# Storing residual tiles later, and two units in seven products for two more up projections, in a two-layer hybrid trunk

## The chip, the cores and the metric

The kernel runs on one core of a Trainium2 chip. The metric is the time of one execution on the device in microseconds (us). A measurement is the median of several runs; the profile is of one further execution, taken by the hardware profiler.

## The reference

Two layers work on 256 tokens of width 2048, all in float32. Each layer normalises x, projects it to queries, keys, values, the two halves of a spatial gating unit and two sets of gates, runs sliding-window attention and the gating unit, projects both to the model width, merges them with the gates, projects once more and adds the result to x. Then comes a gated feed-forward block of width 5632, added to x as well:

```python
for l in range(DEPTH):
    h = rms_norm(x, mix_norm[l])
    proj = h @ w_in[l]
    q, k, v, uv, gate_logits = jnp.split(proj, cuts, axis=-1)
    ...
    merged = gates[..., :D_MODEL] * branch_a + gates[..., D_MODEL:] * branch_b
    x = x + merged @ w_out[l]
    h2 = rms_norm(x, ffn_norm[l])
    x = x + (jax.nn.silu(h2 @ w_gate[l]) * (h2 @ w_up[l])) @ w_down[l]
```

## The kernel before

**Precision.** TensorE multiplies in a rounded format, so each operand is split into a high part (the rounded value) and a low part (the remainder), and a product is three matmuls: high by high (L399), weight's low by activation's high (L400), weight's high by activation's low (L401). For a weight block of 256 rows by 512 columns, ScalarE makes the high part (`whi`, L256) and VectorE the low part (`wlo`, L264). The activations are stored transposed in four units of 512 rows (`uh`, `ul`).

**Jobs and steps.** A job is one product of all 256 tokens with 1024 weight columns (two halves of 512, c = 0 and c = 1). It goes over its units; a whole step is one weight block against both token tiles, 12 matmuls, so a unit has 4 steps, 48 matmuls. The first `m` units of a job instead take a Strassen-like scheme: seven products of 6 matmuls, 42 in all. It costs four subtractions of weight blocks (L240, VectorE), seven high and seven low parts in place of four, and sums of activation blocks (`sh`, `sl`), which a unit has only if it was made with `sums`. `HEAD` says which products come first in a job (five for m = 1, nine for m = 2: 11a, 11b, t1a, t1b, t2a, t2b, 21a, t3a, t3b), `TAIL` which are mixed into the whole steps, and `SUM_AT` how many steps ahead of the job each subtraction is made.

**The order of the work** is written out by hand: nothing is scheduled by the compiler, and every engine takes its instructions in the order in which the program emits them. `Stream.next` keeps the high parts up to six and the low parts up to five blocks ahead of TensorE, emits the subtractions when their step has come, and emits the load of a weight buffer (1 MB, SP's queue, L220) as soon as the blocks of the buffer five loads earlier have been used. `after(n, fn)` puts work n steps later; a whole step counts 1, a product 0.5. `evicting` empties the accumulators behind a job's half, the second token tile some steps later, which depends through `behind` on the `m` of the next job.

**Residuals and norms.** `residual` (L967 on) runs two jobs whose halves are the four tiles of x, each 256 by 512. Each tile is fetched ahead (`fetch_x`, SP's queue, L356); behind its half VectorE adds the product to it (L995 or L997) and the tile is stored to DRAM for the next residual (`keep_x`, 512 KB, SP's queue, L359), 7 steps behind the first half of a job or 8 behind the second. Where a norm follows (both output projections, and the last down round of layer 0), the tile also becomes a unit of the next stage: VectorE transposes it in blocks (L483), POOL issues 16 gathers of 32 KB (L489, at most eight under way), ScalarE scales what has landed (L583) and makes its high part (L587, or L511 and L523 with sums), VectorE its low part (L590). The gathers of one tile stand behind those of the tile before on POOL's queue.

**The feed-forward block** has three rounds over hidden tiles 0 to 3, 4 to 7 and 8 to 10. A round takes a gate and an up job for each pair of hidden tiles (named by the pair's first tile: gate 0, up 0, gate 2, up 2 and so on), then two down jobs. The gate's half is evicted by ScalarE (L1088), the up half by VectorE (L1094), which multiplies both; the hidden tile is then transposed by the same gathers. Gate 2, 4, 6 and 8 have m = 2, gate 0 and all up and down jobs m = 1. Where this text numbers a layer's jobs, gate 0 follows the second job of the output projection. All larger tiles share 25 buffers (`N_BIG`).

Of the kernel before, what the change touches and what calls it, by code (L numbers as in the profile page):

```python
# [37 lines left out]
N_BIG = 25  # L38
G_BUSY, G_LAND = 3.5, 3
T1_LATE, THEN_LATE, UNIT_LATE = (1.5, 3), (3, 7), (3, 3)  # L40
Q_FIRST = 15
Q_STEP = 4
LOAD_BY = (1, 2, 3, 4)
ROUNDS = ((0, 1, 2, 3), (4, 5, 6, 7), (8, 9, 10))
M_OUT, M_FFN, M_DOWN = (0, 1), (2, 1, 1), 1
M_Q = 0
M_GATE, M_ATT, M_SGU = (1, 1, 1, 1), (0, 0), (1, 0)
M_V, M_U = 1, 1
# [4 lines left out]
def hybrid_trunk(ctx: ExitStack, tc: tile.TileContext, x, mix_norm, w_in, q_norm, k_norm, sinks,  # L53
# [106 lines left out]
    for l in range(DEPTH):  # L160
        wl = w_in[l]
        for o in (0, None)[::-1 if l == 0 else 1]:
            add_job([wl[:, o:o + CW2]], m=M_Q * l) if o is not None else add_job([wl[:, O_KV:O_KV + CW]])
        for o, m in ((O_V, M_V), (O_U, M_U), (O_GATE, M_GATE[0]), (O_GATE + CW2, M_GATE[1])):
            add_job([wl[:, o:o + CW2]], m=m)
        add_job([wl[:, O_GATE + D:O_GATE + D + CW2]], m=M_GATE[2])
        for i, o in enumerate((0, CW2)):
            add_job([w_attn_branch[l, :, o:o + CW2]], m=M_ATT[i])
        add_job([wl[:, O_GATE + D + CW2:O_GATE + 2 * D]], m=M_GATE[3])
        for i, o in enumerate((0, CW2)):  # L170
            add_job([w_sgu_branch[l, :, o:o + CW2]], m=M_SGU[i])
        for i, o in enumerate((0, CW2)):
            add_job([w_out[l, :, o:o + CW2]], m=M_OUT[i])
        for fs in ROUNDS:
            for f in fs[::2]:
                if f + 1 < NF:
                    for w, m in zip((w_gate, w_up), M_FFN if f else (1, 1)):
                        add_job([w[l, :, f * CW:(f + 2) * CW]], m=m)
                else:
                    add_job([w[l, :, f * CW:(f + 1) * CW] for w in (w_gate, w_up)], m=M_FFN[2])  # L180
            for o in (0, CW2):
                add_job([w_down[l, :, o:o + CW2]], units=list(fs), m=M_DOWN)

    needed = {}
    for i, n in uses:
# [109 lines left out]
    def after(n, fn):  # L295
        steps.append((slot_no[0] + n, fn))
# [61 lines left out]
    def keep_x(c):  # L358
        nc.sync.dma_start(rows(kept[c]), xt[c])  # L359
        home[c] = kept[c]  # L360
# [608 lines left out]
    def residual(units, nxt, sums, out_at=None, scale=None):  # L969

        for j in range(0, NCH, 2):

            def done(c, ps, j=j):
                o = j + c

                square_at = 5 if c == 0 else behind(2, 2, 5)

                def then():
                    nxt.unit(o, sums=o < sums)
                    after(square_at, lambda: nxt.squares(o))  # L980
                    if o == NCH - 1:
                        after(square_at + 1, lambda: nxt.finish())

                evicting(c, lambda t: added(o, t, ps), then if nxt is not None else None, late_then=UNIT_LATE)
                if out_at is None:
                    after(7 if c == 0 else 8, lambda: keep_x(o))

            def added(o, t, ps):
                n = 2 if out_at is not None and o == NCH - 1 else 1
                w = CW // n  # L990
                for i in range(n):
                    sl = slice(i * w, (i + 1) * w)
                    d, src = xt[o][:, t, sl], ps[t][:, sl]
                    if scale is None:
                        nc.vector.tensor_tensor(out=d, in0=src, in1=d, op=ALU.add)  # L995
                    else:
                        nc.vector.scalar_tensor_tensor(out=d, in0=src, scalar=scale, in1=d, op0=ALU.mult, op1=ALU.add)  # L997
                    if out_at is not None:
                        eng = nc.sync if i == 0 else nc.scalar
                        eng.dma_start(out_at[0, t * P:(t + 1) * P, o * CW + i * w:o * CW + (i + 1) * w], d)  # L1000

            job = jobs[job_no[0]]
            length = 3.5 * job.m + 4 * (len(job.units) - job.m)
            after(length - 8, lambda j=j: fetch_x(j))
            after(length - 6, lambda j=j: fetch_x(j + 1))
            run(units, done)
# [3 lines left out]
    for l in range(DEPTH):  # L1010

        pl = layer[l]
        parameters(pl)
        kv = slot([P, NT, CW], name="kv")
        qs = [slot([P, NT, CW], name="q") for _ in range(2)]
        att, spa = Attention(pl), Spatial(pl, norm)

        def scaled_into(c, dst, ps):
            evicting(c, lambda t: None,
                     ahead=lambda t: nc.scalar.activation(dst[:, t, :], ps[t], AF.Copy, scale=norm.r[t]))  # L1020

        def kv_done(c, ps):
            scaled_into(0, kv, ps)
            att.keys(kv)
            if l:
                att.begin()

        def q_done(c, ps):
            scaled_into(c, qs[c], ps)
            att.queries(c, qs[c])  # L1030
            if c == 1 and not l:
                att.begin()

        after(2, lambda unit=norm.units[0]: add_sums(unit))
        for done in (kv_done, q_done)[::-1 if l else 1]:
            run(norm.units, done)
        run(norm.units, spa.v)
        run(norm.units, spa.u)

        ga, gb, mT = [None] * NCH, [None] * NCH, [None] * NCH  # L1040

        def gate(dst, j):
            def done(c, ps):
                dst[j + c] = slot([P, NT, CW], name="gate")
                def tanh(t):
                    nc.scalar.activation(dst[j + c][:, t, :], ps[t], AF.Tanh, scale=norm.rh[t])

                evicting(c, lambda t: None, ahead=tanh)
            run(norm.units, done)

        def branch(dst, j, units, then=None):
            def done(c, ps):
                d = dst[j + c]

                def then_():
                    then(j + c)
                    transposed(mT, j + c, ga[j + c], sums=j + c == 0)

                evicting(c, lambda t: nc.vector.scalar_tensor_tensor(out=d[:, t, :], in0=d[:, t, :], scalar=1.0,
                                                                     in1=ps[t], op0=ALU.add, op1=ALU.mult),  # L1060
                         then_ if then is not None else None)
            run(units, done)

        def merge(j):
            nc.vector.tensor_tensor(out=flat(ga[j]), in0=flat(ga[j]), in1=flat(gb[j]), op=ALU.add)

        for j in (0, 2):
            gate(ga, j)
        gate(gb, 0)
        for j in (0, 2):  # L1070
            branch(ga, j, att.attT)
        after(SGU_SUMS, lambda unit=spa.sguT[0]: add_sums(unit))
        gate(gb, 2)
        for j in (0, 2):
            branch(gb, j, spa.sguT, merge)

        norm = Norm(ffn_cols(l))
        residual(mT, norm, max(M_FFN), scale=0.5)

        nxt = Norm(mix_cols(l + 1)) if l + 1 < DEPTH else None  # L1080
        for i, fs in enumerate(ROUNDS):
            hid, hT = {}, {}

            def gate_done(f, c, ps):
                hid[f] = a = slot([P, NT, CW], name="hid")

                evicting(c, lambda t: None,
                         ahead=lambda t: nc.scalar.activation(a[:, t, :], ps[t], AF.Silu, scale=norm.r[t]))  # L1088

            def up_done(f, c, ps):  # L1090
                a = hid[f]

                def upped(t):
                    nc.vector.scalar_tensor_tensor(out=a[:, t, :], in0=ps[t], scalar=norm.r[t], in1=a[:, t, :],  # L1094
                                                   op0=ALU.mult, op1=ALU.mult)

                evicting(c, upped, lambda: transposed(hT, f, a, on_pe=f == NF - 1, sums=f in fs[:M_DOWN]))

            for f in fs[::2]:
                if f + 1 < NF:  # L1100
                    run(norm.units, lambda c, ps: gate_done(f + c, c, ps))
                    run(norm.units, lambda c, ps: up_done(f + c, c, ps))
                else:
                    run(norm.units, lambda c, ps: (gate_done, up_done)[c](f, c, ps))
            if i == len(ROUNDS) - 1:
                if nxt is not None:
                    prepare(l + 1)
                residual(hT, nxt, M_Q, out if nxt is None else None)
            else:
                residual(hT, None, 0)  # L1110
        norm = nxt
# [37 lines left out]
```

## Time and profile before

| | |
|---|---|
| median of 3 runs | 2463.84 us (2461.32 to 2466.27) |
| the profiled execution | 2466.55 us |
| its span, first to last instruction | 2464.6 us |
| granted TensorE clock, mean | 0.997 |
| TensorE matmuls, of them in jobs | 10950, 10404 |
| VectorE busy | 1990.1 us, 81% |
| ScalarE busy | 1429.3 us, 58% |
| read from and written to HBM | 492.04 MB, 16.78 MB |

In the views of the profile PE is TensorE, DVE VectorE, ACT ScalarE, POOL GpSimd and SP SyncE; a `q` behind an engine is its queue. A line of a timeline has the start and the duration in us, engine, line, operation, what it writes and reads, how many alike follow each other, and in brackets how long the engine was idle before it and what ended that. A matmul is shown as 0.39 us long, but they overlap: one begins every 0.227 us. A line of the windows has, for a stretch A:B, its length, the busy time of each engine with the number of its instructions, the granted clock as a share of full speed (PEclk), the busy share of the 16 DMA engines and GB/s. "to landing" is the time from the issue of a DMA to the arrival of all its data.

### The profile page before, as it was taken

How to read it: one execution, taken by the hardware profiler on the slowest of the kernel's cores; microseconds unless marked ns; L12 is line 12 of the kernel's file. 1: busy time of each engine (PE TensorE's matmuls, PEld its weight loads, DVE VectorE, ACT ScalarE, POOL GpSimd, SP SyncE). 2: the span in 40 equal slices, each digit the busy share in tenths (PEclk: the TensorE clock that was granted, in tenths of full speed). 3: DMA queues.
4: the chain of work that ended last, by engine and by line, in shares of the span. 5: the costliest groups of instructions: out<-in, count | busy, mean ns of one | idle time of the engine just before them, and what ended most of it. 6: DMA issues, size and time to landing. Idle time of an engine off the chain costs nothing. (4 is left out here: it accounts for less than half of the span.)

```text
span 2464.6 us, 30889 instructions
## 1 busy us (share of the span) xinstructions
PE 2443.4 (99%) x10950; PEld 2012.3 (82%) x10950; DVE 1990.1 (81%) x2189; ACT 1429.3 (58%) x1758; POOL 475.0 (19%) x903
## 2 busy tenths in 40 slices
PE   9999999999999999999999999999999999999999
PEld 7888888877888888888888888887778888888887
DVE  7898768786978797788879976777869787978786
ACT  6575545475655665465666665554756555655653
POOL 1421300441220022002235022014402200220020
PEclk9999999999999999999999999999999999999999
DMA  8555556776576757666776546566856757575764
GB/s 311 195 202 190 165 188 218 225 251 216 213 242 205 256 197 243 226 248 198 267 262 218 184 165 201 190 202 205 284 197 222 239 194 263 209 238 190 260 205 166
DMA packets 179051, 539.20 MB, mean 219 GB/s; under 512 B 23872, under 2 KB 26544, under 8 KB 178896
## 3 DMA queue, kind: packets, MB, share of 16 engines
q1 hardware_dynamic: 150832, 508.51, 60.5%
q0 software_dynamic: 27744, 28.44, 3.8%
q8 instruction: 86, 1.41, 0.2%
q14 instruction: 69, 0.57, 0.1%
q10 hardware_dynamic: 320, 0.27, 0.0%
HBM read 492.04 MB, written 16.78 MB: 206 GB/s over the span
## 5 line engine op out<-in xcount | busy, mean ns | idle before, releaser
L264 DVE TENSOR_TENSOR wlo<-raw,whi 128x1024 fp32r<-128x1024 f32 (+1 forms) x956 | 1150.5, 1219 | 381.6 <-PE acc L400 278.6
L256 ACT ACTIVATE whi<-raw 128x1024 fp32r<-128x1024 f32 (+1 forms) x956 | 997.2, 1057 | 692.8 <-PE acc L401 611.9
L399 PE MATMUL acc<-whi,uh 128*128 128x512 f32 x3004 | 1178.0, 392 | 6.8 <-ACT uh L587 4.2
L400 PE MATMUL acc<-wlo,uh 128*128 128x512 f32 x3004 | 1171.1, 390 | 2.4 <-DVE wlo L264 2.4
L401 PE MATMUL acc<-whi,ul 128*128 128x512 f32 x3004 | 1171.7, 390 | 1.4 <-DVE ul L590 1.2
L489 POOL DMA_DIRECT2D tt<-blk x800 | 392.1, 497 | 1682.6 <-DVE blk L483 665.4
L399 PEld LDWEIGHTS acc<-whi,uh 128*128 128x128 f32 x3004 | 565.1, 188 | 128.9 <-ACT uh L587 5.5
L401 PEld LDWEIGHTS acc<-whi,ul 128*128 128x128 f32 x3004 | 565.0, 188 | 121.4 <-DVE ul L590 3.3
L400 PEld LDWEIGHTS acc<-wlo,uh 128*128 128x128 f32 x3004 | 565.2, 188 | 119.8 <-DVE wlo L264 4.0
L399 PE MATMUL acc<-whi,sh 128*128 128x512 f32 x464 | 182.4, 393 | 2.8 <-ACT acc L435 2.2
L256 ACT ACTIVATE whi<-sum 128x1024 fp32r<-128x1024 f32 x116 | 122.8, 1058 | 102.1 <-PE acc L401 87.0
L400 PE MATMUL acc<-wlo,sh 128*128 128x512 f32 x464 | 181.6, 391 | 0.0
L401 PE MATMUL acc<-whi,sl 128*128 128x512 f32 x464 | 181.4, 391 | 0.0
L264 DVE TENSOR_TENSOR wlo<-sum,whi 128x1024 fp32r<-128x1024 f32 x116 | 141.3, 1218 | 6.1 <-PE acc L400 6.1
L399 PEld LDWEIGHTS acc<-whi,sh 128*128 128x128 f32 x464 | 87.5, 188 | 25.7 <-ACT acc L435 6.6
L435 ACT ACTIVATE acc<-acc 128x512 f32<-128x512 f32 x150 | 88.4, 589 | 28.7 <-PE acc L401 20.2
L401 PEld LDWEIGHTS acc<-whi,sl 128*128 128x128 f32 x464 | 87.5, 189 | 18.4
L400 PEld LDWEIGHTS acc<-wlo,sh 128*128 128x128 f32 x464 | 87.5, 189 | 18.0 <-DVE wlo L264 0.3
L590 DVE TENSOR_TENSOR ul<-tt,uh 128x1024 fp32r<-128x1024 f32 x36 | 44.0, 1223 | 42.8 <-ACT uh L587 37.6
L240 DVE TENSOR_TENSOR raw<-raw,sum 128x1024 f32<-128x1024 f32 x58 | 71.0, 1225 | 2.0
L240 DVE TENSOR_TENSOR sum<-raw,raw 128x1024 f32<-128x1024 f32 x58 | 71.0, 1224 | 1.4
L240 DVE TENSOR_TENSOR sum<-raw 128x1024 f32<-128x1024 f32 x58 | 70.7, 1219 | 0.0
(126 smaller groups left out, 1044.5 us busy)
## 6 DMA issues: line engine op xcount, KB each, us to landing
raw<-in_w_in_dram SPq DMA_DIRECT2D x112, 1024.0 KB, 5.5
raw<-in_w_down_dram SPq DMA_DIRECT2D x88, 1024.0 KB, 6.3
raw<-in_w_gate_dram SPq DMA_DIRECT2D x80, 1024.0 KB, 6.3
raw<-in_w_up_dram SPq DMA_DIRECT2D x80, 1024.0 KB, 6.4
raw<-in_w_out_dram SPq DMA_DIRECT2D x32, 1024.0 KB, 6.9
tt<-blk POOLq DMA_DIRECT2D x800, 32.0 KB, 4.9
raw<-in_w_attn_branch_dram SPq DMA_DIRECT2D x16, 1024.0 KB, 6.0
raw<-in_w_sgu_branch_dram SPq DMA_DIRECT2D x16, 1024.0 KB, 5.7
```

Of the source, the lines that this page charges most:

```text
L240: nc.vector.tensor_tensor(out=self.raw(dst), in0=self.raw(one), in1=self.raw(two), op=ALU.subtract)
L256: nc.scalar.activation(hi[:, k, :], raw[:, k, :], AF.Copy)
L264: nc.vector.tensor_tensor(out=lo[:, k, :], in0=raw[:, k, :], in1=hi[:, k, :].bitcast(F32), op=ALU.subtract)
L399: nc.tensor.matmul(ps, a, hi, start=first, stop=False, skip_group_check=True)
L400: nc.tensor.matmul(ps, a, lo, start=False, stop=False, skip_group_check=True)
L401: nc.tensor.matmul(ps, b, hi, start=False, stop=last, skip_group_check=True)
L435: nc.scalar.activation({"11": x, "t2": e, "t3": y}[name], a, AF.Copy)
L489: nc.gpsimd.dma_start(blocks(d)[:, :, i] if whole else d[:, i].rearrange("p k t c -> p (k t) c"), src)
L590: nc.vector.tensor_tensor(out=blocks(unit.lo), in0=tv, in1=blocks(unit.hi).bitcast(F32), op=ALU.subtract)
```

## The change

Two things change. `keep_x` is emitted 20 steps behind the addition instead of 7 or 8 where a norm follows (`nxt is not None`): 4 tiles at each output projection and at the last down round of layer 0, 12 stores of 28. And the up jobs of pairs 2 and 6 get m = 2 in place of 1, in both layers. `M_DOWN` becomes a table of ones, which says the same as the 1 before; `max(M_FFN)`, which sets how many units of the feed-forward norm have sums, stays 2.

```diff
+KEEP_LATE = 20
...
-M_OUT, M_FFN, M_DOWN = (0, 1), (2, 1, 1), 1
+M_OUT, M_FFN, M_DOWN = (0, 1), (2, 2, 1), ((1, 1), (1, 1), (1, 1))
+UP_TWO = (2, 6)
...
-        for fs in ROUNDS:
+        for fs, ms in zip(ROUNDS, M_DOWN):
             for f in fs[::2]:
                 if f + 1 < NF:
-                    for w, m in zip((w_gate, w_up), M_FFN if f else (1, 1)):
+                    for w, m in ((w_gate, M_FFN[0] if f else 1), (w_up, M_FFN[1] if f in UP_TWO else 1)):
                         add_job([w[l, :, f * CW:(f + 2) * CW]], m=m)
                 else:
                     add_job([w[l, :, f * CW:(f + 1) * CW] for w in (w_gate, w_up)], m=M_FFN[2])
-            for o in (0, CW2):
-                add_job([w_down[l, :, o:o + CW2]], units=list(fs), m=M_DOWN)
+            for o, m in zip((0, CW2), ms):
+                add_job([w_down[l, :, o:o + CW2]], units=list(fs), m=m)
...
                 if out_at is None:
-                    after(7 if c == 0 else 8, lambda: keep_x(o))
+                    after(KEEP_LATE if nxt is not None else 7 if c == 0 else 8, lambda: keep_x(o))
...
-                evicting(c, upped, lambda: transposed(hT, f, a, on_pe=f == NF - 1, sums=f in fs[:M_DOWN]))
+                evicting(c, upped, lambda: transposed(hT, f, a, on_pe=f == NF - 1, sums=f in fs[:max(M_DOWN[i])]))
```

## The prediction

> **What bounds the kernel now.** I read the page first, for the share of each engine; then the windows of one job after another; then the waits inside the only long job; last the timelines of the engines and of SP's queue around that wait.
>
> ```profile
> span 2464.6 us, 30889 instructions
> ...
> PE 2443.4 (99%) x10950; PEld 2012.3 (82%) x10950; DVE 1990.1 (81%) x2189; ACT 1429.3 (58%) x1758; POOL 475.0 (19%) x903
> ```
>
> TensorE is the bound almost everywhere. A job's first matmul is found by counting matmuls in the kernel's own order (12 for a whole step, 6 for a product), which gives windows that are exactly one job long: gate 0, up 0, gate 2 and up 2 of layer 0, and gate 0 of layer 1.
>
> ```profile
> core 0: us, PE busy (x) PEld busy (x) DVE busy (x) ACT busy (x) POOL busy (x), PEclk, DMA share, GB/s
> 535.07:586.20 51.13, 46.75 (x188) 36.83 (x187) 38.92 (x44) 32.00 (x45) 17.54 (x34) 0.93 0.62 206
> 586.20:628.43 42.23, 42.23 (x188) 34.84 (x186) 32.93 (x31) 22.68 (x25) 1.10 (x3) 1.00 0.58 199
> 628.43:669.23 40.80, 40.80 (x182) 33.80 (x180) 40.70 (x42) 28.40 (x31) 14.62 (x30) 1.00 0.65 233
> 669.23:711.46 42.23, 42.23 (x187) 34.84 (x186) 31.58 (x30) 22.68 (x25) 1.10 (x3) 1.00 0.60 199
> ...
> 1759.05:1810.50 51.45, 46.86 (x188) 36.48 (x187) 39.29 (x45) 31.85 (x45) 17.44 (x34) 0.93 0.61 204
> ```
>
> Gate 2 has two units in seven products (14 x 6 + 8 x 12 = 180 matmuls) and takes 40.80 us, 0.2267 us a matmul; TensorE never waits, although VectorE is busy for 40.70 of those 40.80 us. Up 0 and up 2 have one such unit (7 x 6 + 12 x 12 = 186). Gate 0 has 186 too, but takes 51.13 and 51.45 us: 186 x 0.2267 = 42.16, so 9.0 and 9.3 us are lost in it, at a granted clock of 0.93. Here the end of the job is set by something else than TensorE.
>
> ```profile
> 570.42 0.39 PE L401 MATMUL acc<-whi,ul 128*128 128x512 f32 x1
> 572.82 0.50 PE L399 MATMUL acc<-whi,uh 128*128 128x512 f32 x1 [2.01 <-ACT uh L587]
> ...
> 574.67 0.63 PE L399 MATMUL acc<-whi,uh 128*128 128x512 f32 x1
> 575.10 0.63 PE L400 MATMUL acc<-wlo,uh 128*128 128x512 f32 x1
> ```
> ```profile
> 569.97 1.71 ACT L583 ACTIVATE tt<-tt,vcols 128x256 f32<-128x256 f32 x4 [6.22 <-DMA tt<-blk]
> ```
> ```profile
> 522.39 1.71 ACT L583 ACTIVATE tt<-tt,vcols 128x256 f32<-128x256 f32 x4 [4.16 <-DMA tt<-blk]
> ```
> ```profile
> 525.09 1.23 DVE L264 TENSOR_TENSOR wlo<-raw,whi 128x1024 fp32r<-128x1024 f32 x1 [2.80 <-ACT whi L256]
> ```
>
> TensorE reaches the last unit of gate 0 just after 570.4 and starts on it at 572.82. It waited for that unit's high part, ScalarE made it as soon as the 16 gathers of the last residual tile had landed (569.97, after 6.22 us of idleness), and after the stall about ten matmuls come 0.43 us apart instead of 0.2267: another 2 us. The stalls early in gate 0 make up the rest; they come from VectorE being late, and it lost 2.80 us at 525.09 because ScalarE stood, in order, behind the gathers of the tile before (4.16 us at 522.39). So gate 0 is bound by the chain addition, transposition, gathers, split.
>
> **The change part by part. The products.** Up 2 and up 6 of both layers get a second unit in seven products: 4 units x (48 - 42) matmuls x 0.2267 us = 5.4 us less TensorE time; the rows for gate 2 and up 2 say the same (42.23 - 40.80 = 1.4 a job). The activation sums that this needs exist already for units 0 and 1. What is added is weight work: per job four subtractions (L240) and three low parts (L264) on VectorE, three high parts on ScalarE. ScalarE has room (22.68 of 42.23 us busy). VectorE has 42.23 - 31.58 = 10.6 us idle in up 2 against seven more operations; what matters is when.
>
> ```profile
> 617.59 1.23 DVE L264 TENSOR_TENSOR wlo<-raw,whi 128x1024 fp32r<-128x1024 f32 x1 [0.36 <-PE acc L400]
> ```
> ```profile
> 634.15 4.63 DVE L264 TENSOR_TENSOR wlo<-raw,whi 128x1024 fp32r<-128x1024 f32 x4
> ```
> ```profile
> 653.42 2.35 DVE L264 TENSOR_TENSOR wlo<-raw,whi 128x1024 fp32r<-128x1024 f32 x2
> 655.69 1.22 DVE L508 TENSOR_TENSOR sl<-sums,sh 128x1024 fp32r<-128x1024 f32 x1
> ```
> ```profile
> 661.37 1.22 DVE L264 TENSOR_TENSOR wlo<-raw,whi 128x1024 fp32r<-128x1024 f32 x1
> ```
>
> The first low part of gate 2 ends at 618.8, 9.6 us ahead of its use at 628.43; by the seventh product (which begins six products of 1.36 us later, at 636.59) the first of the four at 634.15 ends at 635.4, 1.2 us ahead. A head of nine products thus eats 8.4 us of lead. Up 2 starts with only 669.23 - 662.6 = 6.6 us, because gate 2 in front of it keeps VectorE full. By that alone it would fall 1.8 us short. But the head of gate 2 also carries four evictions and two transpositions of the hidden tile, and behind a gate job the eviction is ScalarE's. So I walk VectorE's own queue in the new order from the second low part of the row at 653.42 (it starts at 654.55), at the pitch of (655.69 - 653.42) / 2 = 1.135 us. Between it and the low part of the seventh product stand two low parts of gate 2, eight subtractions, six low parts of the head and two operations of the hidden unit (the row at 655.69 and one more): 18 operations, so it starts 19 pitches later, at 654.55 + 19 x 1.135 = 676.1, by estimate 0.25 later for the two subtractions that overwrite what was just read, and ends 1.22 on, at 677.6. It is used by the second matmul of a product that begins at 669.23 + 6 x 1.36 = 677.4, so at 677.6 too. The margin is nil. I take 0.25 us a job, 1.0 us in all. Bounds: nothing (it can't gain, up 2 waits for nothing now); or, with the full 1.22 us an operation, 19 x 0.085 = 1.6 us a job, 6.5 in all. Later there is slack again: whole steps last 2.72 us against one operation. The second half of the gate's eviction moves from 0.5 to 2 steps behind on ScalarE; the bank is touched again only after nine products (12.2 us), so it costs nothing.
>
> **The stores.** Twelve stores move: those of both output projections, and of the last down round of layer 0. The first two tiles of each had steps 7 and 8 after their addition, in the second half's job; at 20 they fall into the next stage. The last two had steps 7 and 8 in gate 0; at 20 they fall into up 0, where no gather runs. In gate 0 the order on SP's queue was:
>
> ```profile
> 541.79 6.11 SPq L220 DMA_DIRECT2D raw<-in_w_gate_dram  x3
> 552.18 2.64 SPq L220 DMA_DIRECT2D raw<-in_w_up_dram  x2
> 554.87 0.46 SPq L359 DMA_DIRECT2D kept<-x  x1
> 560.47 0.37 SPq L220 DMA_DIRECT2D raw<-in_w_up_dram  x1
> 560.89 0.46 SPq L359 DMA_DIRECT2D kept<-x  x1
> ```
>
> The new steps are 2.5 and 4.5 of gate 0: the stores of tiles 0 and 1 will stand behind the third of the first three loads (about 548) and between the two at 552.18. So gate 0 does not lose its two stores, it has two others 7 to 8 us earlier. The job before it (493 to 535) does lose two and gets none. The stores wait for nothing (their additions are 50 us old) and hold nothing up on SP but the loads behind them.
>
> ```profile
> 505.00:524.00 19.00, 19.00 (x86) 15.73 (x85) 13.91 (x15) 11.51 (x20) 7.86 (x16) 1.00 1.02 372
> 524.00:541.00 17.00, 16.14 (x70) 12.76 (x69) 15.81 (x19) 11.37 (x13) 0.84 (x2) 1.00 0.30 107
> 541.00:571.00 30.00, 28.82 (x119) 23.05 (x117) 22.41 (x28) 17.98 (x29) 16.70 (x33) 0.94 0.92 307
> ```
> ```profile
> L489 POOL DMA_DIRECT2D tt<-blk x32: 496/496/498, 540.2 to 562.3; - x32
> ...
> DMA to landing us min/median/max: 1.7/5.5/7.8
> ```
>
> While the gathers run the DMA engines are full (1.02 and 0.92). At 372 GB/s a store of 512 KB is 1.4 us of them. [...] In gate 0 the gathers of both tiles (the last answer) took 5.5 us at the median and 7.8 at most; the very last, issued at 562.3 behind the store of 560.89, freed ScalarE at 569.97, 7.6 us on. Without that store I take 1.4 off it, one store's time. Against that, the stores now ahead of the earlier gathers: 0.6. And a shorter stall leaves fewer slow matmuls: half of the 2 us, 1.0. Together 1.0 + 1.4 - 0.6 + 1.0 = 2.8 us a layer, 5.6 in all, of 18.3 that are lost there now. Bounds a layer: the whole loss of 9, or worse than now (last rival). In layer 1's first projection one small stall has the same cause:
>
> ```profile
> 1234.47 1.23 DVE L590 TENSOR_TENSOR ul<-tt,uh 128x1024 fp32r<-128x1024 f32 x1 [2.68 <-ACT uh L587]
> ```
> ```profile
> 1239.81 0.50 PE L399 MATMUL acc<-whi,uh 128*128 128x512 f32 x1 [0.79 <-DVE x L995]
> ```
>
> VectorE waits 2.68 us for a gathered tile and is then 0.79 us late with an addition; two stores less ahead of that gather should end most of it: 0.7.
>
> The sum: -5.4 + 1.0 - 5.6 - 0.7 = -10.7 us. The profiled execution took 2466.55 us (span 2464.6), 2.7 above the median 2463.84 of the three runs; its 2455.8 stands for a median of 2453.1. What a measurement of this kernel can tell from no change is about 0.2%, 4.9 us.
>
> **Rivals.** First, stores do not slow gathers at all. For: the median from issue to landing is the same for the 16 gathers of tile 0 (no store beside them) and of tile 1 (two stores), by the view of DMA issues for 493.8 to 504.5 and for 505.3 to 516.5:
>
> ```profile
> tt<-blk POOLq DMA_DIRECT2D x16, 32.0 KB, 5.6
> ```
> ```profile
> tt<-blk POOLq DMA_DIRECT2D x16, 32.0 KB, 5.7
> ```
>
> [...] Against: the last gather behind a store took 7.6 us, not 5.6. Then only -5.4 + 1.0 = -4.4 is left: 2459.4. [...] Chance 0.20.
>
> Second, VectorE becomes the bound at the heads of up 2 and up 6. For: it is full in gate 2 (40.70 of 40.80 us) and the margin above is nil. Against: the walk finds no deficit. With 1.6 us lost a job, 6.5, it gives -5.4 + 6.5 - 6.3 = -5.2, and with 2 us of slow matmuls after two of the four stalls, 4 more, -1.2: 2462.6. Chance 0.14.
>
> Third, slower: the two stores in gate 0 stand ahead of the gathers of tile 2, 2.8 us of DMA time; ScalarE, in order, waits longer at that tile with the weights' high parts queued behind it, TensorE stalls at unit 2, and tile 3's gathers, behind on POOL's queue, come 2.8 later too. With 2 us of slow matmuls more, 4.8 a layer: 9.6 - 5.4 + 1.0 = +5.2, 2469.0. It decides once tile 2 lands over 2.5 us later against TensorE's arrival than now. For: the engines are full there. Against: these gathers are mostly issued before the first store. Chance 0.08.
>
> The residual tiles also keep their share of the 25 common buffers some 12 steps longer; a wait on the store itself would show that, and I have no price for it but those above.
>
> **How the numbers follow.** The forecast has 0.58. The low end of the range takes 6 us a layer in gate 0 and a free head: -5.4 - 12 - 0.7 = -18.1, 2446. The high end is the second rival's, 2463. Faster by over 0.2%: the forecast nearly whole and under half of the first rival, 0.67; slower 0.10; within 0.2% the rest, 0.23.
>
> **What would show it.** Right: up 2 and up 6 last 40.8 to 41.1 us each; gate 0 some 48 us at a clock above 0.93; ScalarE's wait for the second gathered tile below 4.16 us; the last unit's gathers landing earlier after gate 0's start than the 34.9 us of now. Wrong: low-part waits of TensorE (L400 for wlo) in up 2 beyond 0.5 us; a stall at unit 2 of gate 0 with a later landing of tile 2; a gate 0 unchanged at 51 us, which would leave the products alone.

## The result and the profile after

The changed kernel takes 2452.56 us, the median of four runs (2451.49 to 2453.18), against 2463.39 (2461.32 to 2466.27) of the kernel before, now with a fourth run: a ratio of 0.9955 with a 95% interval of 0.9938 to 0.9972, 10.8 us faster. The prediction said 2453.1, in a range of 2446 to 2463. The profiled execution took 2453.18 us, 13.4 less than the one profiled before.

First the page of the changed kernel, whose lines stand two higher than before from the new constants on (L399 is now L401, L264 is L266, L587 is L589, L590 is L592):

```profile
span 2451.4 us, 30927 instructions
...
PE 2432.1 (99%) x10926; PEld 2003.7 (82%) x10926; DVE 2019.0 (82%) x2217; ACT 1442.8 (59%) x1770; POOL 473.3 (19%) x903
```

24 matmuls fewer, 28 VectorE operations and 12 ScalarE operations more: the four units. Then the same jobs as in the prediction, gate 0, up 0, gate 2 and up 2 of layer 0 and gate 0 of layer 1, in the view of windows:

```profile
535.41:582.89 47.48, 43.91 (x188) 34.42 (x186) 39.06 (x44) 31.62 (x45) 16.77 (x34) 1.00 0.64 222
582.89:625.09 42.20, 42.20 (x188) 34.83 (x186) 32.92 (x31) 22.68 (x25) 1.10 (x3) 1.00 0.64 224
625.09:665.89 40.80, 40.80 (x182) 33.78 (x180) 40.70 (x42) 28.73 (x31) 14.61 (x30) 1.00 0.65 233
665.89:706.85 40.96, 40.96 (x182) 33.70 (x180) 38.63 (x37) 25.91 (x28) 1.10 (x3) 1.00 0.56 206
1750.88:1799.19 48.31, 43.95 (x188) 34.37 (x187) 39.12 (x44) 31.67 (x45) 16.80 (x34) 1.00 0.62 218
```

Gate 0 went from 51.13 to 47.48 us and in layer 1 from 51.45 to 48.31, its clock from 0.93 to 1.00; up 2 went from 42.23 to 40.96. Up 0 now writes two of the stores (224 GB/s in place of 199) and is no longer for it. Now the end of gate 0, in the timelines of ScalarE and of TensorE:

```profile
568.22 1.71 ACT L585 ACTIVATE tt<-tt,vcols 128x256 f32<-128x256 f32 x4 [4.73 <-DMA tt<-blk]
```
```profile
570.16 0.39 PE L403 MATMUL acc<-whi,ul 128*128 128x512 f32 x1
571.07 0.50 PE L401 MATMUL acc<-whi,uh 128*128 128x512 f32 x1 [0.52 <-ACT uh L589]
571.41 0.40 PE L402 MATMUL acc<-wlo,uh 128*128 128x512 f32 x1
572.33 0.50 PE L403 MATMUL acc<-whi,ul 128*128 128x512 f32 x1 [0.53 <-DVE ul L592]
572.67 0.40 PE L401 MATMUL acc<-whi,uh 128*128 128x512 f32 x1
572.90 0.39 PE L402 MATMUL acc<-wlo,uh 128*128 128x512 f32 x1
```

ScalarE still stands behind the last tile's gathers, 4.73 us instead of 6.22, and TensorE still waits for the last unit's high part, but 0.52 us instead of 2.01. Behind the stall the matmuls come 0.23 us apart; before, they came 0.43 apart. SP's queue in gate 0 has the new order that was read off the code:

```profile
542.28 6.11 SPq L222 DMA_DIRECT2D raw<-in_w_gate_dram  x3
548.44 0.46 SPq L361 DMA_DIRECT2D kept<-x  x1
552.68 0.37 SPq L222 DMA_DIRECT2D raw<-in_w_up_dram  x1
553.10 0.51 SPq L361 DMA_DIRECT2D kept<-x  x1
554.95 11.66 SPq L222 DMA_DIRECT2D raw<-in_w_up_dram  x3
```

Summing the gaps between the matmuls of gate 0 beyond 0.227 us shows where its time came from. A gap of 0.38 to 0.5 us is counted as a slow matmul, one of 0.5 or more as a stall:

| gate 0 | job | slow matmuls, early | slow matmuls, after the last unit's stall | lost in stalls |
|---|---|---|---|---|
| layer 0, before | 51.13 | 8: 1.6 us | 6: 1.2 us | 5.6 us |
| layer 0, after | 47.48 | 0 | 0 | 4.6 us |
| layer 1, before | 51.45 | 0 | 11: 2.2 us | 6.6 us |
| layer 1, after | 48.31 | 0 | 0 | 5.3 us |

So the slow matmuls gave more than the stalls. The early eight of layer 0 follow stalls that did not change (gaps of 1.1 and 1.4 us in both kernels); the same eight come back in layer 0 in two of the experiments, so they are an accident of that profile and not the change's gain (what stood ahead of them follows under the slow matmuls). Without them gate 0 gave 2.0 and 3.1 us. With 4.8 for the four up jobs and 1.1 for layer 1's first projection (44.63 to 43.52) that is 11.0, against 10.8 by the medians. The agreement is better than the account: all jobs together differ by 13.6 us between these two profiles. One more job belongs to the change: layer 1's first output projection went from 45.70 to 44.59 us. It lasts 44.55 to 44.59 in the profiles of all five kernels with further products (this one and four of those below) and 45.04 to 46.07 in the nine without; no forecast had it, and why it does so stays open.

### The profile page after: what moved, and what is told of

It is laid out like the page before. It is cut to its first block, busy times and chain, and to the rows that moved or that the text cites. A ratio compares the mean times of both kernels' runs of the same rounds, so it can differ in the third digit from the quotient of the medians.

```text
span 2451.4 us, 30927 instructions
## 1 busy us (share of the span) xinstructions
PE 2432.1 (99%) x10926; PEld 2003.7 (82%) x10926; DVE 2019.0 (82%) x2217; ACT 1442.8 (59%) x1770; POOL 473.3 (19%) x903
## 5 line engine op out<-in xcount | busy, mean ns | idle before, releaser
L266 DVE TENSOR_TENSOR wlo<-raw,whi 128x1024 fp32r<-128x1024 f32 (+1 forms) x960 | 1153.9, 1218 | 346.4 <-PE acc L402 247.5
L401 PE MATMUL acc<-whi,uh 128*128 128x512 f32 x2964 | 1160.4, 391 | 3.4 <-ACT uh L589 1.7
L402 PE MATMUL acc<-wlo,uh 128*128 128x512 f32 x2964 | 1154.4, 389 | 2.8 <-DVE wlo L266 2.8
L403 PE MATMUL acc<-whi,ul 128*128 128x512 f32 x2964 | 1154.4, 389 | 2.2 <-DVE ul L592 2.1
L401 PEld LDWEIGHTS acc<-whi,uh 128*128 128x128 f32 x2964 | 556.5, 188 | 123.0 <-ACT uh L589 2.8
L403 PEld LDWEIGHTS acc<-whi,ul 128*128 128x128 f32 x2964 | 556.4, 188 | 120.1 <-DVE ul L592 3.8
L401 PE MATMUL acc<-whi,sh 128*128 128x512 f32 x496 | 194.0, 391 | 3.2 <-ACT acc L437 2.5
L402 PE MATMUL acc<-wlo,sh 128*128 128x512 f32 x496 | 193.3, 390 | 0.0
L403 PE MATMUL acc<-whi,sl 128*128 128x512 f32 x496 | 193.2, 389 | 0.0
L266 DVE TENSOR_TENSOR wlo<-sum,whi 128x1024 fp32r<-128x1024 f32 x124 | 150.6, 1217 | 5.2 <-PE acc L402 5.2
L401 PEld LDWEIGHTS acc<-whi,sh 128*128 128x128 f32 x496 | 93.1, 188 | 26.5 <-ACT acc L437 6.0
L402 PEld LDWEIGHTS acc<-wlo,sh 128*128 128x128 f32 x496 | 93.1, 188 | 19.3 <-DVE wlo L266 0.3
L437 ACT ACTIVATE acc<-acc 128x512 f32<-128x512 f32 x150 | 88.3, 589 | 30.1 <-PE acc L403 21.8
L242 DVE TENSOR_TENSOR raw<-raw,raw 128x1024 f32<-128x1024 f32 x62 | 75.5, 1218 | 0.0
```

What stands on the lines that cost most here:

```text
L242: nc.vector.tensor_tensor(out=self.raw(dst), in0=self.raw(one), in1=self.raw(two), op=ALU.subtract)
L266: nc.vector.tensor_tensor(out=lo[:, k, :], in0=raw[:, k, :], in1=hi[:, k, :].bitcast(F32), op=ALU.subtract)
L401: nc.tensor.matmul(ps, a, hi, start=first, stop=False, skip_group_check=True)
L402: nc.tensor.matmul(ps, a, lo, start=False, stop=False, skip_group_check=True)
L403: nc.tensor.matmul(ps, b, hi, start=False, stop=last, skip_group_check=True)
L437: nc.scalar.activation({"11": x, "t2": e, "t3": y}[name], a, AF.Copy)
```

## The experiments

My theory: the two edits work apart; the stores act through the gathers of the last tile in gate 0, where a stall also costs the half-speed matmuls behind it, and partly through the job before gate 0. The rivals: stores do not slow gathers; VectorE binds in the heads of up 2 and 6. Each kernel was timed beside the kernel before, whose median stands behind `against`; edits are against the changed kernel unless said.

### Each edit alone

```diff
-UP_TWO = (2, 6)
+UP_TWO = ()
```

> Only the later stores; up 2 and up 6 keep one unit in seven products. If the stores are what shortened the two gate 0 jobs (51.1 and 51.4 us before, 47.5 and 48.3 after the whole change) and the small stall in layer 1's first projection, these jobs last about 47.5 to 48.3 us here too and the kernel is 6 to 9 us faster than before, 2455 to 2457. If gathers do not care about stores (the first rival), gate 0 stays at 51 us and the time within 1 us of before. Up 2 and up 6 should last 42.2 us.

2458.31 against 2465.18, 0.9977 (0.9969 to 0.9986): -6.9 us.

```diff
-after(KEEP_LATE if nxt is not None else 7 if c == 0 else 8, lambda: keep_x(o))
+after(7 if c == 0 else 8, lambda: keep_x(o))
```

> Only the products; stores 7 and 8 steps behind as before. If the two edits add up, this is 4.8 us faster than before (four up jobs of 41.0 to 41.6 us instead of 42.2), 2458.5, with gate 0 at 51 us in both layers. If the products had a part in the shorter gate 0 jobs, these are shorter here as well and it is faster than that. If VectorE were the bound behind two such jobs in a row, up 2 and up 6 would last over 42 us.

2461.56 against 2465.18, 0.9990 (0.9982 to 0.9999): -3.6 us. That is less than the 4.8 expected, which lies just beyond the interval's end of 4.4. Together the two make -10.5 against the change's -10.8, so the edits add up within their intervals. The windows are those of gate 0 and up 2 of layer 0, of the stores alone and then of the products alone:

```profile
535.31:582.73 47.42, 45.05 (x187) 35.66 (x186) 38.63 (x44) 31.72 (x45) 17.94 (x34) 0.96 0.65 222
665.75:707.98 42.23, 42.23 (x188) 34.83 (x186) 31.57 (x30) 22.71 (x25) 1.10 (x3) 1.00 0.59 199
```
```profile
536.13:587.17 51.04, 45.51 (x188) 35.51 (x186) 38.59 (x44) 31.38 (x45) 17.09 (x34) 0.97 0.63 206
670.18:711.15 40.97, 40.97 (x182) 33.72 (x180) 38.63 (x37) 25.93 (x28) 1.10 (x3) 1.00 0.56 206
```

Gate 0 is shorter with the stores' edit alone (47.42 us) and not with the products' (51.04); up 2 the other way round.

### Which stores, and out of what

Only the last two stores of each stage late (nothing stored in gate 0, the job before as it was); only the first two late (four stores in gate 0); none stored at all. From here on every kernel that doesn't name `UP_TWO` has the first of these edits too, so that it has the stores' part alone:

```diff
-UP_TWO = (2, 6)
+UP_TWO = ()
...
-after(KEEP_LATE if nxt is not None else 7 if c == 0 else 8, lambda: keep_x(o))
+after(KEEP_LATE if nxt is not None and j else 7 if c == 0 else 8, lambda: keep_x(o))
```

> Products as before; only the last two tiles of each of the three residuals are stored 20 steps behind, the first two 7 and 8 steps as before. Gate 0 then has no store at all, the job before it has two as before. If what counts is that the last tile's gathers have no store beside them, gate 0 is at least as short as with the whole change: 44 to 47.5 us, and the kernel 7 to 13 us faster than before. If what counts is the job before gate 0 (no stores there), gate 0 stays near 51 us. If stores do not matter, nothing moves.

2458.04 against 2465.18, 0.9976 (0.9967 to 0.9985): -7.1 us, the same as with all stores late.

```diff
+after(KEEP_LATE if nxt is not None and not j else 7 if c == 0 else 8, lambda: keep_x(o))
```

> Products as before; only the first two tiles are stored 20 steps behind, the last two 7 and 8 steps as before. Gate 0 then has four stores, the job before it none: the suspected cost doubled. If stores slow the gathers in gate 0, it is longer than before, 52.5 to 56 us, by one to two stores' 1.4 us each and slow matmuls, and the kernel 0 to 8 us slower than before. If what counts is the job before gate 0, gate 0 is shorter than 51 us and the kernel faster. If stores do not matter, nothing moves.

2460.08 against 2465.18, 0.9979 (0.9970 to 0.9987): -5.1 us. Twice the stores in gate 0, and still faster than the kernel before: my theory, by which each store ahead of the gathers has its price, does not give this.

```diff
-if out_at is None:
-    after(KEEP_LATE if nxt is not None else 7 if c == 0 else 8, lambda: keep_x(o))
+if out_at is None and nxt is None:
+    after(7 if c == 0 else 8, lambda: keep_x(o))
```

> Products as before; the twelve stores are left out altogether, so the next residual adds to an older x (its time is the same otherwise). This is the most that moving the stores can give. By the runs so far the last tile's gathers start about 1.1 us earlier against gate 0 when the job before has no store, and take 15.2 us instead of 17.8 when gate 0 has none: arrival 31.3 us after gate 0's start instead of 34.7, which leaves no stall at the last unit; gate 0 then 45 to 46 us, the kernel 10 to 12 us faster than before. If the two gains cannot be had together (either half alone already gave 47 to 48 us), gate 0 stays at 47 us and the kernel is 7 us faster, like the later stores alone.

2454.60 against 2465.25, 0.9963 (0.9950 to 0.9977): -10.7 us without any product, so the stores had more to give than the change took. The answers on the gathers of the last tile in layer 0, of the kernel before and of the one without stores:

```profile
L489 POOL DMA_DIRECT2D tt<-blk x16: 496/496/498, 551.6 to 562.3; - x16
...
DMA to landing us min/median/max: 4.0/5.7/7.8
```
```profile
L491 POOL DMA_DIRECT2D tt<-blk x16: 496/496/498, 553.0 to 563.4; - x16
...
DMA to landing us min/median/max: 3.4/4.8/6.6
```

Here the median moves too, from 5.7 to 4.8 us, and the maximum from 7.8 to 6.6.

### Both pairs of stores out of gate 0, and four up jobs

All four stores in up 0, with the products of the change (`UP_TWO` stays (2, 6)):

```diff
-after(KEEP_LATE if nxt is not None else 7 if c == 0 else 8, lambda: keep_x(o))
+after((KEEP_LATE if j else 34) if nxt is not None else 7 if c == 0 else 8, lambda: keep_x(o))
```

> The whole change, but the first two tiles are stored 34 steps behind instead of 20, so that all four stores fall into the first steps of up 0 and neither gate 0 nor the job before it has one. If stores beside the gathers are what costs, gate 0 is as short as with no stores, 45 to 46 us, and the kernel 2 to 4 us faster than the changed one, 2448 to 2451. If the two stores early in gate 0 cost nothing, it is the changed kernel's 2452 to 2453. If tiles held so long run short of buffers, a wait on the stores shows and it is slower.

2449.89 against 2465.25, 0.9939 (0.9926 to 0.9953): -15.4 us. Gate 0 of layer 0 takes 45.03 us in the windows, and in the timeline ScalarE waits 3.22 us for the last tile:

```profile
536.62:581.65 45.03, 43.43 (x188) 34.53 (x186) 37.82 (x43) 31.20 (x44) 16.81 (x34) 1.00 0.63 211
```
```profile
566.97 1.71 ACT L585 ACTIVATE tt<-tt,vcols 128x256 f32<-128x256 f32 x4 [3.22 <-DMA tt<-blk]
```

The changed kernel's stores, and four up jobs of a layer with two units in seven products:

```diff
-UP_TWO = (2, 6)
+UP_TWO = (2, 4, 6, 8)
```

> The whole change, with two units in seven products for up 4 and up 8 as well. VectorE is less full in gate 4 and gate 8 (0.86) than in gate 2 and gate 6 (1.00), so their heads should have lead: each of the four jobs 40.8 to 41.0 us instead of 42.2, 5 to 5.6 us off the changed kernel, 2447. If back-to-back pairs cost VectorE its lead after all, the jobs last over 41.5 us and little is won.

2447.16 against 2465.25, 0.9934 (0.9921 to 0.9947): -18.1 us, where the changed kernel had -10.8 beside its own kernel before; the two medians themselves are 5.4 us apart. The windows of up 2 and up 4 of layer 0:

```profile
666.03:706.99 40.96, 40.96 (x182) 33.71 (x180) 38.62 (x37) 25.92 (x28) 1.10 (x3) 1.00 0.57 206
832.11:872.91 40.80, 40.80 (x182) 33.78 (x180) 38.01 (x36) 25.80 (x28) 1.35 (x3) 1.00 0.56 208
```

Up 4 loses nothing at its head.

### The price of the clock

Against the kernel before: eight matmuls into an unused accumulator, ahead of the last unit's first whole step in gate 0, fill the stall and change nothing else.

```diff
+if job_no[0] in GATE0 and u == 3 and left == [2, 2]:
+    pd = ps_at.tile([P, CW], F32, tag="at", name=nm("dummy"))
+    for i in range(8):
+        nc.tensor.matmul(pd, units[2].hi[:, 0, :P], hi[:, 0, :], start=True, stop=True)
...
+GATE0 = (15, 46)
```

> The kernel before, with eight extra matmuls into an unused bank just ahead of the last unit of gate 0 in both layers (1.8 us of TensorE, beside the wait of 2.2 us there). The result is untouched. If the slow matmuls behind that stall come from TensorE having been idle, they go: gate 0 loses about 2 us in each layer, 49 us, and the kernel is 3 to 4 us faster than before although it does more work. If the clock has another cause, the ten slow matmuls stay and nothing is won or up to 1 us a layer lost.

2463.10 against 2465.25, 0.9994 (0.9985 to 1.0002): by the medians 2.2 us faster, which this measurement can hardly tell from nothing and which is below what was expected. The profile is plainer. TensorE's timeline in layer 0:

```profile
571.06 1.98 PE L446 MATMUL dummy<-whi,uh 128*128 128x512 f32 x8
572.88 0.39 PE L400 MATMUL acc<-whi,uh 128*128 128x512 f32 x1
573.11 0.40 PE L401 MATMUL acc<-wlo,uh 128*128 128x512 f32 x1
```

The unit's first matmul comes when it came before (572.88; 572.82 before), yet no slow matmuls follow: gate 0 takes 49.38 and 49.03 us, 1.8 and 2.4 less than before, of which the slow matmuls are 1.2 and 2.2. (Layer 0 has the early eight here, as before.) Elsewhere the profile gives some back: up 2 of layer 1 lasts 43.91 us in place of 42.69.

### Where the stores of gate 0 stand

The first pair where the last pair was stored before; the first pair there beside the last pair; and one store alone, with the last gathers:

```diff
+after((23, 24, KEEP_LATE, KEEP_LATE)[o] if nxt is not None else 7 if c == 0 else 8, lambda: keep_x(o))
```

> Products as before. Tiles 0 and 1 are stored 23 and 24 steps behind, which is 5.5 and 8.5 steps into gate 0, where the kernel before stores tiles 2 and 3; tiles 2 and 3 go 20 steps behind, into up 0. So gate 0 is as before, and only the job before it has lost its stores. If the place of the stores in gate 0 is what counts, tile 3's gathers take 17 to 18.5 us from first issue to last landing, as before, and gate 0 lasts 49.5 to 51 us. If emptying the job before is what counts, gate 0 lasts 47 to 48 us, as in the changed kernel.

2464.21 against 2466.10, 0.9997 (0.9987 to 1.0006). The job before gate 0 is empty of stores, gate 0 has its two where it always had them, and nothing is gained; ScalarE's wait in layer 0 is 7.70 us:

```profile
571.04 1.70 ACT L585 ACTIVATE tt<-tt,vcols 128x256 f32<-128x256 f32 x4 [7.70 <-DMA tt<-blk]
```

```diff
+after((23, 24, 7, 8)[o] if nxt is not None else 7 if c == 0 else 8, lambda: keep_x(o))
```

> Products as before. Tiles 0 and 1 are stored 23 and 24 steps behind and tiles 2 and 3 7 and 8, so four stores stand at 5.5 and 8.5 steps into gate 0, two at each place, none in the job before. Two stores there cost tile 3's gathers 2.8 us against none (17.6 against 14.8 us). If the cost goes with the bytes, four make it 20 us, gate 0 lasts 52 to 54 us and the kernel is 2 to 5 us slower than before. If only the fact of a store ahead of the last gathers counts, it stays at 17 to 18.5 us and gate 0 at 50 to 51.

2458.53 against 2466.10, 0.9968 (0.9955 to 0.9980): two stores more at the same two places, and faster. (In layer 0 the fourth is issued at 26.7 us after gate 0's start, just behind the last gather at 26.4.)

```diff
+after((34, 34, KEEP_LATE, 8)[o] if nxt is not None else 7 if c == 0 else 8, lambda: keep_x(o))
```

> Products as before. Of the four stores only tile 3's stands in gate 0, 8 steps behind as before (8.5 steps into gate 0); tiles 0, 1 and 2 fall into up 0. Tile 3's gathers took 14.8 us with no store in gate 0, 17.6 with two at 5.5 and 8.5 steps, and, unlike bytes would have it, 16.9 with four there. If the last store, issued just ahead of the last gathers, is what costs, they take 16.5 to 17.6 here and gate 0 lasts 48 to 51 us. If the first of the two (or both together) is needed, they stay at 15 and gate 0 at 45 to 47.

2460.19 against 2464.53, 0.9983 (0.9972 to 0.9993). The two layers differ: in layer 0 the last gather is issued 1.4 us behind the store and the tile's gathers last 17.55 us, in layer 1 at the same moment as the store and they last 15.22. But most of that difference is older than the store: from the first to the last issue the gathers took 10.9 us in layer 0 and 9.1 in layer 1. The cleaner comparison is layer 0 of the kernel with only the last two stores late, which has no store in gate 0 and issues the gathers at the same times (17.2 to 28.0 us after gate 0's start; 17.1 to 28.0 here). Two gathers stand behind the store. The view of DMA issues, for these two alone, and the timeline of ScalarE, first with the store and then without:

```profile
tt<-blk POOLq DMA_DIRECT2D x2, 32.0 KB, 6.9
```
```profile
570.35 1.71 ACT L585 ACTIVATE tt<-tt,vcols 128x256 f32<-128x256 f32 x4 [6.01 <-DMA tt<-blk]
```
```profile
tt<-blk POOLq DMA_DIRECT2D x2, 32.0 KB, 4.7
```
```profile
566.87 1.71 ACT L585 ACTIVATE tt<-tt,vcols 128x256 f32<-128x256 f32 x4 [3.82 <-DMA tt<-blk]
```

In this pair of profiles the last two gathers land 2.2 us later with one store ahead of them, 34.66 in place of 32.43 us after gate 0's start.

All placements together, in us; the third column is from the first issue to the last landing of the last tile's 16 gathers:

| kernel | stores in gate 0, us from its start (layer 0) | gathers of the last tile, layers 0 / 1 | gate 0, layers 0 / 1 |
|---|---|---|---|
| before | 19.8, 25.8 | 18.28 / 17.31 | 51.1 / 51.4 |
| first pair late in its place | 19.8, 26.0 | 19.50 / 17.78 | 52.1 / 50.4 |
| one, last | 26.6 | 17.55 / 15.22 | 49.5 / 46.4 |
| four, late | 19.3, 19.8, 25.6, 26.7 | 17.25 / 16.50 | 47.8 / 49.8 |
| only first two late (four) | 12.0, 16.6, 18.9, 24.8 | 16.34 / 16.72 | 46.5 / 49.4 |
| after | 13.0, 17.7 | 16.29 / 16.97 | 47.5 / 48.3 |
| none, only last two late | none | 15.21 / 15.14 | 47.2 / 48.1 |
| none, all in up 0 | none | 15.03 / 14.79 | 45.0 / 46.8 |
| none, the twelve left out | none | 14.04 / 14.41 | 46.3 / 46.8 |

Without a store the gathers last 14.0 to 15.2 us. Against 15.0 a pair lengthens them by 1.3 to 2.0 us where it stands early (after) and by 2.3 to 4.5 where it stands late (before, and the first pair in its place). Two more kernels have the late pair, the products alone (18.46 / 17.06) and the filled one (17.76 / 16.80), which widens its range to 1.8 to 4.5, so the two ranges touch. Four do not cost more than two. Gate 0's own length also holds slow matmuls, so the gathers are the better column to compare.

### Both improvements

```diff
-UP_TWO = (2, 6)
+UP_TWO = (2, 4, 6, 8)
-after(KEEP_LATE if nxt is not None else 7 if c == 0 else 8, lambda: keep_x(o))
+after((KEEP_LATE if j else 34) if nxt is not None else 7 if c == 0 else 8, lambda: keep_x(o))
```

> The two versions that beat the changed kernel, together: two units in seven products in up 2, 4, 6 and 8, the first two tiles stored 34 steps behind, the last two 20. If the edits stay independent, as they were so far: 2452.6 less 2.7 (stores) less 5.4 (products), 2444.5; gate 0 at 45 to 47 us, the four up jobs at 40.8 to 41.0. If fuller up jobs and the stores that now fall into up 0 meet, less.

2444.16 against 2466.10, 0.9911 (0.9897 to 0.9926): 21.9 us below the kernel before, where the changed kernel was 10.8 below; the medians of the two are 8.4 apart.

## Why the prediction was right, step by step

**The products: right.** Forecast -5.4 with 0.25 us a job lost at the head. Up 2 and up 6 last 40.96 to 41.00 us in layer 0 and 41.60 and 41.01 in layer 1, against 40.80 without a loss. So up 2 of layer 1 is outside the 40.8 to 41.1 that was to show it; 0.6 of its 0.8 us are a wait for an accumulator that ScalarE copies (L437) and not for VectorE, and the kernel before loses half a microsecond in the same job (42.69 in place of 42.2). The walk along VectorE's queue can be checked: gate 2 began 3.34 us earlier than before, which moves the walk's 676.35 to 673.01. VectorE and TensorE in the changed kernel:

```profile
673.03 2.35 DVE L266 TENSOR_TENSOR wlo<-raw,whi 128x1024 fp32r<-128x1024 f32 x2
```
```profile
674.05 0.39 PE L401 MATMUL acc<-whi,uh 128*128 128x512 f32 x1
674.30 0.50 PE L402 MATMUL acc<-wlo,uh 128*128 128x512 f32 x1
674.64 0.40 PE L403 MATMUL acc<-whi,ul 128*128 128x512 f32 x1
674.88 0.39 PE L401 MATMUL acc<-whi,uh 128*128 128x512 f32 x1
```

The first of the two low parts at 673.03 is the seventh product's; it ends at 674.25, and the matmul that uses it starts at 674.30. From 674.05 to 674.88 three matmuls take 0.83 us in place of 0.68, which is the 0.16 lost in this job: the margin was nil, as said. The second rival (VectorE becomes the bound) had the right place and no price.

**Gate 0 as a whole: right.** 2.8 us a layer were forecast; 3.65 and 3.14 came, 2.0 and 3.1 without the accident of the early eight. The terms behind it held less well.

**The job before gate 0: not shown.** Forecast: 1.0 us a layer from fewer stores there, the first term of the 2.8; it was my estimate, and no run shows it. ScalarE's wait for the second tile, which was to fall below 4.16 us, is 4.03:

```profile
522.89 1.31 ACT L585 ACTIVATE tt<-tt,vcols 128x256 f32<-128x256 f32 x3 [4.03 <-DMA tt<-blk]
```

The median of that tile's gathers stays where it was, 5.8 us after 5.7, now without a store beside them (the view of DMA issues, 506 to 517):

```profile
tt<-blk POOLq DMA_DIRECT2D x16, 32.0 KB, 5.8
```

Its last landing lies 12.62 and 12.59 us ahead of gate 0 (12.78 and 12.52 before); over all kernels the mean is 12.2 with stores in that job and 12.7 without, in a scatter from 11.1 to 13.8. So half a microsecond at most is likely and none is excluded, as with the first pair late in the last pair's place, which gained nothing. The stalls early in gate 0 did not shrink. The prediction had the equal medians in this job and set them aside because of one late gather in another; for this job they were the better guide.

**The last gather without its store, and the stores ahead of the earlier ones: right in direction.** Net 0.8 was forecast. The last landing moved from 34.80 and 34.13 us after gate 0's start to 32.71 and 33.47: 2.1 and 0.7 earlier, and the stalls of gate 0 shrank by 1.0 and 1.2. The first rival, that stores do not slow gathers, falls in gate 0: without stores the median is 4.8 in place of 5.7. The equal medians of the job before speak for that rival and these against it; what tells the two jobs apart was not found.

**The slow matmuls: mis-sized.** I took half of 2 us, because the stall would only shorten. They went altogether (1.2 us in layer 0, where the prediction had read about ten and 2 us, and 2.2 in layer 1), and filling the stall was worth 1.8 and 2.4. Over the thirteen kernels with nothing filled in, the six gates whose last unit came 2.4 us or more after the matmul before it all had 3 to 11 slow ones behind; of six at 1.5 to 2.2 us two did; below that there was no run of them. The granted clock shows what lies around them. Windows of the kernel before, around the two groups of slow matmuls in layer 0:

```profile
539.85:543.26 3.41, 1.69 (x7) 1.03 (x7) 3.41 (x4) 0.80 (x2) 3.10 (x7) 1.00 0.34 61
543.26:546.67 3.41, 3.41 (x9) 2.67 (x10) 3.41 (x5) 2.91 (x5) 2.76 (x6) 0.50 0.93 330
570.57:573.98 3.41, 0.97 (x4) 0.30 (x2) 1.18 (x2) 3.38 (x6) 0.00 (x0) 1.00 0.29 119
573.98:577.40 3.42, 3.32 (x8) 2.65 (x9) 3.42 (x4) 1.63 (x2) 0.00 (x0) 0.50 0.34 50
```

The clock is halved for 3.41 us at a time (once for twice that, from 1795.95), and within a trace these stretches start on one grid: 543.26 and 573.98 are nine times 3.413 us apart. From one run to the next the grid moves against the kernel: counted from the span's start it goes through 3.96 us in the trace of the kernel before and through 5.27 in that of the changed one. In gate 0 of the fourteen traces there are twelve such stretches. In the grid's window ahead of each only two to six matmuls began (six, two and five in the kernel before), where fifteen fit at 0.227 us. In the traces of the kernel before and of the changed one no window at full clock with seven or more was followed by half a clock; one with five (2458.14, before) was not either. So what goes with the half clock in these traces is the number of matmuls that begin in one window of the grid, and not the length of a stall: two stalls of 1.1 and 1.4 us, in a window with six matmuls, stood ahead of the early eight, and the 2.19 us ahead of layer 0's last unit in the kernel with one late store were followed by no slow matmul. One profile does not tell how often a given stall costs a halved stretch.

**Layer 1's first projection:** 0.7 forecast, 1.1 measured; its stall of 0.79 us is gone. That wait is 0.05 to 1.26 us in the four profiles with stores in the job before it and at most 0.20 in the ten without, so the cause holds and the size varies.

**The third rival** (stores ahead of tile 2's gathers) can be seen and does not decide. In the timeline of the changed kernel a small stall is there at unit 2:

```profile
559.83 0.50 PE L403 MATMUL acc<-whi,ul 128*128 128x512 f32 x1 [0.48 <-DVE ul L592]
```

Tile 2 lands at 20.2 us after gate 0's start (20.07 and 19.66 before; in layer 0 there was no such stall), and the last unit's arrival sets the end anyway.

So the sum held because what the job before gate 0 did not give, the clock gave in its place, and that is luck: the total is right to 0.5 us, two of its terms are not, and the clock's part is another one in another run.

Why four stores cost the gathers no more than two stays open, but the traces narrow it. In every kernel the last weight load ahead of the last gather is issued 24.3 to 26.7 us after gate 0's start, stores or none, so leaving a store out did not bring the next load forward here. The last gather lands within 1.2 us of that load (32.71 and 32.88 us after gate 0's start in layer 0 of the changed kernel, 34.80 and 34.09 before). From 16 us after gate 0's start to the last landing the windows show 286 to 306 GB/s without a store, 312 to 345 with a pair and 358 to 372 with four. Layer 0, the first pair late in the last pair's place and then four late:

```profile
551.20:570.94 19.74, 18.68 (x81) 14.55 (x79) 12.29 (x16) 8.13 (x14) 8.96 (x18) 1.00 0.96 312
550.79:567.82 17.03, 16.50 (x71) 13.01 (x71) 11.85 (x16) 7.64 (x13) 9.50 (x18) 1.00 1.01 360
```

Four stores add bytes, but more was moved per microsecond, and what allowed that is not shown.

## What to carry to other kernels

Where an in-order engine waits for a row of small gathers, read the last landing as well as the median, and move other traffic out of that window altogether rather than earlier in it (gate 0 of layer 0 took 51.1 us with the pair of stores late in it, 47.5 with a pair early and 45.0 with all four in up 0). A stall of TensorE can cost more than its length: here each window of 3.41 us at full clock that was followed by a stretch at half clock had at most six matmuls begun in it, of fifteen. The change gained 1.2 and 2.2 us more than its shorter stalls in this way, and one profile does not say how often that comes; look for the 0.50 in the granted clock of several. Whether VectorE can feed one more product can be settled beforehand by walking its queue at the measured pitch (1.135 us here: the walk gave 673.01, the trace 673.03).

## What was unexpected of the hardware

Back-to-back VectorE operations on 128x1024 each show 1.22 us but start 1.135 apart (653.42 to 655.69 in the kernel before), which the walk needed to be right. The first gather of the last tile was issued 29.0 to 29.4 us after the second tile's last landing in every kernel, whatever the stores did. And twice the stores at the same two places (four late) gave shorter gathers than one pair (17.25 against 19.50 us in layer 0, 16.50 against 17.78 in layer 1; 17.76 to 18.46 and 16.80 to 17.31 in the three kernels with the pair of before).
